# Spreading the operand sums of a Strassen product over the products of the pair before, in one layer of a hybrid decoder

## Chip, core and metric

The kernel runs on one core of a Trainium2 chip. The metric is device time in microseconds, the median of the runs.

## What is computed

One layer of a decoder trunk on 1024 tokens of width 1024, all in float32: two head groups (retention and a delta-rule mixer) behind one input projection, an output projection, a gated feed-forward network, a gated embedding and a final norm. The change lies in the feed-forward part, cut here to what matters:

```python
x = x + mixed @ w_o[i]
hf = rms_norm(x, norm_ffn_w[i])
x = x + (jax.nn.silu(hf @ w_gate[i]) * (hf @ w_up[i])) @ w_down[i]
hp = rms_norm(x, norm_ple_w[i])
x = x + (p[i] @ w_ple_up[i]) * jax.nn.sigmoid(hp @ w_ple_gate[i])
```

The hidden width is 2816, 22 tiles of 128.

## The kernel before

Activations lie transposed, feature by token, in two token halves of 512. For float32 accuracy each operand of a matmul is split into a high part (a copy by ScalarE into the matmul type, L247) and a low part (the operand minus its high part, L248), and every product is three matmuls: high by high, high by low, low by high. Each weight tile is loaded into a stage tile `st` and split into `hi` and `lo`. `dense` (L255) streams the dense projections, of which each step is three matmuls; the function given to it at L1247 says whether VectorE or GpSimd makes the low part of item i.

The feed-forward network of the first token half runs early (`ffn0`) and its hidden tiles go to DRAM (`hd`). For its last two hidden tiles it runs behind the output projection of the second half (`out1`). `norm1` (L1037), called in the evacuation of the first of these gates, takes the norm of the second half: a sum of squares split and multiplied by ones (`nrm`), the square root on ScalarE, the reciprocal on VectorE (L328), and then eight tiles `sq` (L331), each split into `hT1`. `ffn1` then runs gate and up for 22 hidden tiles of the second half.

The product with `w_down` for both token halves is done along the way, two hidden tiles (a pair c) at a time, by Strassen's scheme with seven products, P1 to P7. Its left operands are the four quarter blocks `A` of a pair's `w_down` rows and sums of them (`weights`, L1078, on GpSimd); its right operands are the hidden tiles of the first half, `B[0]` and `B[1]`, loaded from DRAM, those of the second half, `B[2]` and `B[3]`, made by the up products (L1225), and differences of these (`hidden`, L1105, on VectorE; a difference is `sub`, L1076). The split operands lie in eight slots of two `ring` tiles. `unit` (L1119) does a quarter of a product: three matmuls into a PSUM bank `pd`, and an addition by VectorE to the place it belongs to (L1135: `E`, written `rm` in the trace, or the residual `x1`, written `x`). P2, P7 and P3 go on in the bank of the product before them, so their first matmul waits until VectorE has read that bank. For pair 0 ScalarE evacuates P1 and P7 (L1133).

`period` (L1145) lays the units and operands of a pair out in 32 ticks; one tick is taken at each step of `dense`, so that three plain matmuls and three of a product alternate, and the last four ticks hold no product. The 28 units of pair c run in the period of pair c + 1. When the second up product of a pair is done, `hidden(c)` issues all of its differences and splits at once, and the next period begins. `last_period` (L1184) packs the units of the second last pair closer; there `shared` (L1137) adds the sums that several outputs share, behind it `down` multiplies the last pair plainly (L1181) and the gated embedding follows. A scheduler sets the order on each engine from the order in which the program issues instructions and from when their inputs are ready; each engine then works through its own queue in that order.

What the first tick holds, and what a pair ends with:

```python
0: lambda: (dma(out=B[0], in_=hd[f]), dma(out=B[1], in_=hd[f + 1])),
...
while todo:
    tick()
hidden(c)
```

Of the kernel before, what the change touches and what calls it, by code (L numbers as in the profile page):

```python
# [20 lines left out]
KT = 8  # L21
# [85 lines left out]
LEFT = 2  # L107
# [70 lines left out]
def tile_hybrid_layer(ctx: ExitStack, tc: tile.TileContext, I, out):  # L178
# [67 lines left out]
    def split(src, hi, lo, eng=None):  # L246
        act(hi, src, AF.Copy)  # L247
        (eng or V).tensor_tensor(out=lo, in0=src, in1=hi.bitcast(F32), op=ALU.subtract)  # L248
# [81 lines left out]
    def norm_out(raw, w, R, tmp, hi, lo):  # L330
        V.scalar_tensor_tensor(out=tmp, in0=raw, scalar=w, in1=R, op0=ALU.mult, op1=ALU.mult)  # L331
        split(tmp, hi, lo)
# [17 lines left out]
    with ExitStack() as s1:  # L350
# [686 lines left out]
        def norm1():  # L1037
# [3 lines left out]
            for d in range(KT):  # L1041
                norm_out(tail["x1"][d][:, half(1)], pv(NFFN + d), R, tail["sq"](), hT[:, d, 0, :], hT[:, d, 1, :])
# [35 lines left out]
        def weights(c):  # L1078
# [6 lines left out]
            def sums():  # L1085
# [7 lines left out]
                    0: lambda: (dma(out=B[0], in_=hd[f]), dma(out=B[1], in_=hd[f + 1])),  # L1093
                    1: lambda: (part(c, "P1", 0, A[0], G), sums()),
                    3: lambda: sub(G, A[2], A[0], A[2]),
                    5: lambda: part(c, "P2", 0, A[1], G),
                    6: lambda: (part(c, "P1", 1, B[0]), sub(G, A[1], A[1], A[5])),
                    8: lambda: part(c, "P2", 1, B[1]),
# [4 lines left out]
                    26: lambda: part(c, names(c)[6], 0, A[3] if names(c)[6] == "P4" else A[1], G)}  # L1103

        def hidden(c):  # L1105

            B = tail["B"]
            sub(V, B[4], B[2], B[0])
            sub(V, B[5], B[3], B[4])
            part(c, "P6", 1, B[5])  # L1110
            sub(V, B[2], B[3], B[2])
            part(c, "P7", 1, B[2])
            sub(V, B[1], B[5], B[1])
            for n in names(c)[4:]:
                part(c, n, 1, {"P5": B[4], "P3": B[3], "P4": B[1]}[n])

# [20 lines left out]
        def shared(j):  # L1137

            x1, E = tail["x1"], tail["E"]
            V.tensor_tensor(out=E[4 + j], in0=E[4 + j], in1=E[j], op=ALU.add)  # L1140
            V.tensor_tensor(out=x1[j + 4][:, half(0)], in0=x1[j + 4][:, half(0)], in1=E[4 + j], op=ALU.add)
            G.tensor_tensor(out=x1[j][:, half(1)], in0=x1[j][:, half(1)], in1=E[j], op=ALU.add)
            G.tensor_tensor(out=x1[j + 4][:, half(1)], in0=x1[j + 4][:, half(1)], in1=E[4 + j], op=ALU.add)

        def period(c):  # L1145

            ticks = [[] for _ in range(32)]
            if c:
                for u in range(28):
                    ticks[u].append(lambda u=u: unit(c - 1, names(c - 1)[u // 4], u % 4))  # L1150
            for at, fn in weights(c).items():
# [315 lines left out]
```

## Time and profile before

| | |
|---|---|
| median of 3 runs | 1649.02 us (1638.87 to 1649.34) |
| the profiled execution's own time | 1657.07 us |
| its span, first to last instruction | 1655.3 us |
| TensorE matmuls busy | 1511.1 us, 91% |
| VectorE busy | 1240.8 us, 75% |
| ScalarE busy | 729.2 us, 44% |
| GpSimd busy | 532.4 us, 32% |
| DMA, all engines, busiest queue | 36.4% |

Times in the rows are microseconds from the start of the span, unless marked ns. PE is TensorE, DVE VectorE, ACT ScalarE, POOL GpSimd, SP the engine that issues the loads. A name such as `ring<-rm,ring` is what is written and what is read. Idle time before an instruction stands in brackets with what ended it.

### The profile page before, as it was taken

The numbers are of one execution on the slowest core, as the hardware profiler recorded it, in microseconds if no ns is written. First come the engines' busy times: TensorE is split into PE (matmuls) and PEld (weight loads), VectorE is DVE, ScalarE is ACT, GpSimd is POOL, SyncE is SP. The second block draws the span as 40 slices with busy tenths as digits, with TensorE's granted clock in tenths as the row PEclk, the third lists the DMA queues.
The fourth block names the chain that finished last, engine by engine and source line by source line (L and its number), as shares of the span: only waits on it lengthen the run. The fifth ranks groups of instructions, "written<-read, shape, count | busy, mean of one in ns | idle before, by whom it ended". The sixth has DMA issues, their size and how long they took to land.

```text
span 1655.3 us, 21602 instructions
## 1 busy us (share of the span) xinstructions
PE 1511.1 (91%) x7286; PEld 1226.3 (74%) x7286; DVE 1240.8 (75%) x2460; ACT 729.2 (44%) x1451; POOL 532.4 (32%) x404
## 2 busy tenths in 40 slices
PE   6999899998888989889899999999999999998995
PEld 5777778776767767768677777777877777786894
DVE  7669896959798686976855447667777777779877
ACT  6655434434536556263443234533323333333654
POOL 7410111111221123233234314545444445443013
PEclk9999999999999999999999999999999999999997
DMA  6544242334434644243335363322222222322222
GB/s 201 166 169 143 101 132 69 124 115 131 162 117 150 210 152 157 88 142 110 114 123 165 105 189 115 121 90 76 83 77 86 80 76 77 95 72 64 84 74 86
DMA packets 108766, 194.08 MB, mean 117 GB/s; under 512 B 12272, under 2 KB 16496, under 8 KB 108656
## 3 DMA queue, kind: packets, MB, share of 16 engines
q1 hardware_dynamic: 108656, 192.71, 36.4%
q8 instruction: 57, 0.93, 0.2%
q14 instruction: 53, 0.43, 0.1%
HBM read 151.24 MB, written 41.42 MB: 116 GB/s over the span
## 4 chain that ended last, share of the span: by engine, by line
PE 48%; DVE 29%; DMA 8%; ACT 7%; issue 5%; POOL 4%; SPq 0%; DVEq 0%; ACTq 0%; POOLq 0%
PE d L189 26%; PE pd L189 11%; DVE tmp L643 4%; PE pg L189 3%; DVE R L645 3%; POOL lo L248 2%; DVE ring L248 2%; DVE lo L248 2%; DMA st<-in_w_up_dram 1%; DVE rm L1076 1%; ACT hi L247 1%; DMA st<-mixd 1%; DVE Dm L637 1%; DMA st<-in_w_in_dram 1%; DMA st<-in_w_gate_dram 1%
## 5 line engine op out<-in xcount | busy, mean ns | idle before, releaser
L189 PE MATMUL d<-hT,hi 128*128 128x512 f32 x1408 | 460.3, 404 | 9.6 <-DVE g L1011 5.6
L248 POOL TENSOR_TENSOR lo<-st,hi 128x512 fp32r<-128x512 f32 x185 | 261.3, 1414 | 611.2 <-ACT hi L247 552.1
L189 PE MATMUL d<-x,hi 128*128 128x512 f32 x960 | 318.8, 407 | 9.9 <-ACT x L336 8.2
L189 PEld LDWEIGHTS d<-hT,hi 128*128 128x128 f32 x1408 | 266.3, 194 | 62.1 <-ACT hi L247 11.5
L247 ACT ACTIVATE hi<-st 128x512 fp32r<-128x512 f32 x298 | 187.3, 629 | 256.9 <-PE d L189 101.3
L189 PE MATMUL pd<-ring 128*128 128x512 f32 x936 | 270.9, 405 | 26.4 <-DVE rm L1135 23.8
L189 PE MATMUL d<-hT,lo 128*128 128x512 f32 x704 | 281.8, 400 | 2.6 <-POOL lo L248 2.5
L189 PEld LDWEIGHTS pd<-ring 128*128 128x128 f32 x936 | 182.3, 196 | 71.2 <-DVE rm L1135 26.6
L189 PEld LDWEIGHTS d<-x,hi 128*128 128x128 f32 x960 | 176.6, 191 | 44.1 <-ACT x L336 8.2
L189 PE MATMUL d<-x,lo 128*128 128x512 f32 x480 | 192.2, 400 | 2.8 <-POOL lo L248 2.4
L1135 DVE TENSOR_TENSOR x<-x,pd 128x512 f32<-128x512 f32 x200 | 133.5, 683 | 59.4 <-PE pd L189 59.0
L189 PEld LDWEIGHTS d<-hT,lo 128*128 128x128 f32 x704 | 136.2, 193 | 33.4 <-POOL lo L248 4.4
L248 DVE TENSOR_TENSOR lo<-st,hi 128x512 fp32r<-128x512 f32 x113 | 98.5, 872 | 51.2 <-ACT hi L247 50.8
L248 POOL TENSOR_TENSOR ring<-xr,ring 128x512 fp32r<-128x512 f32 x54 | 75.1, 1394 | 182.7 <-ACT ring L247 121.7
L247 ACT ACTIVATE ring<-rm 128x512 fp32r<-128x512 f32 x92 | 57.1, 630 | 145.4 <-PE pd L189 60.3
L189 PEld LDWEIGHTS d<-x,lo 128*128 128x128 f32 x480 | 91.7, 191 | 22.5 <-POOL lo L248 4.3
L643 DVE TENSOR_TENSOR tmp<-Dt,R 128x248 f32<-128x248 f32 (+30 forms) x248 | 88.8, 358 | 3.1
L645 DVE TENSOR_TENSOR R<-R,tmp 128x248 f32<-128x248 f32 (+30 forms) x248 | 86.6, 349 | 3.3
L247 ACT ACTIVATE ring<-xr 128x512 fp32r<-128x512 f32 x54 | 33.6, 628 | 114.6 <-PE pd L189 114.6
L189 PE MATMUL d<-mix,hi 128*128 128x512 f32 x256 | 81.2, 397 | 1.3 <-ACT hi L247 1.3
L248 DVE TENSOR_TENSOR ring<-rm,ring 128x512 fp32r<-128x512 f32 x72 | 74.8, 1073 | 5.5 <-ACT ring L247 4.6
L1135 DVE TENSOR_TENSOR rm<-rm,pd 128x512 f32<-128x512 f32 x72 | 47.6, 681 | 21.5 <-PE pd L189 21.5
(301 smaller groups left out, 2405.2 us busy)
## 6 DMA issues: line engine op xcount, KB each, us to landing
st<-in_w_gate_dram SPq DMA_DIRECT2D x88, 256.0 KB, 2.8
st<-in_w_up_dram SPq DMA_DIRECT2D x88, 256.0 KB, 2.9
st<-in_w_in_dram SPq DMA_DIRECT2D x86, 256.0 KB, 2.8
xr<-in_w_down_dram SPq DMA_DIRECT2D x44, 256.0 KB, 2.6
retd<-rt SPq DMA_DIRECT2D x32, 256.0 KB, 2.7
rr<-retd SPq DMA_DIRECT2D x32, 256.0 KB, 3.3
st<-in_w_o_dram SPq DMA_DIRECT2D x32, 256.0 KB, 2.9
rkvd<-rkvt SPq DMA_DIRECT2D x24, 256.0 KB, 2.1
```

The lines of the kernel that those rows point to most:

```text
L189: return nc.tensor.matmul(ps, lhsT, rhs, start=start, stop=stop, skip_group_check=more)
L247: act(hi, src, AF.Copy)
L248: (eng or V).tensor_tensor(out=lo, in0=src, in1=hi.bitcast(F32), op=ALU.subtract)
L637: V.tensor_tensor(out=Dm, in0=d0v[:, 0].rearrange("p u t -> p t u").unsqueeze(2).broadcast_to([P, 32, 4, NU]), in1=d0v[:, 1].rearrange("p ...
L643: V.tensor_tensor(out=tmp[:, :, 0:i], in0=Dt[:, i:i + 1, 0:i].broadcast_to([P, 8, i]), in1=R[:, :, i:i + 1].broadcast_to([P, 8, i]), op=AL ...
L645: V.tensor_tensor(out=R[:, :, 0:i], in0=R[:, :, 0:i], in1=tmp[:, :, 0:i], op=ALU.subtract)
L1076: eng.tensor_tensor(out=out, in0=x, in1=y, op=ALU.subtract)
L1135: V.tensor_tensor(out=dst, in0=dst, in1=ps, op=ALU.subtract if name == "P4" else ALU.add)
```

## The change

`hidden` returns its parts by tick, and the next period (or, at three quarters of the tick, the last one) issues them between the units. The two hidden tiles of the first half are loaded at ticks 2 and 19 and split at ticks 17 and 28. `shared` is cut in three parts with ticks of their own. In `norm1` GpSimd makes the low part of the seventh tile, and all that period 0 issues on GpSimd is queued behind that instruction (`issue_after`); VectorE and not GpSimd makes the low parts of the weights of the two plain gates and the first gate around it.

```diff
-        (eng or V).tensor_tensor(out=lo, in0=src, in1=hi.bitcast(F32), op=ALU.subtract)
+        return (eng or V).tensor_tensor(out=lo, in0=src, in1=hi.bitcast(F32), op=ALU.subtract)
...
-                norm_out(tail["x1"][d][:, half(1)], pv(NFFN + d), R, tail["sq"](), hT[:, d, 0, :], hT[:, d, 1, :])
+                ins = norm_out(tail["x1"][d][:, half(1)], pv(NFFN + d), R, tail["sq"](), hT[:, d, 0, :], hT[:, d, 1, :], G if d == KT - 2 else V)
+                if d == KT - 2:
+                    tail["held"] = ins.ins
...
-                    0: lambda: (dma(out=B[0], in_=hd[f]), dma(out=B[1], in_=hd[f + 1])),
                     1: lambda: (part(c, "P1", 0, A[0], G), sums()),
+                    2: lambda: dma(out=B[0], in_=hd[f]),
...
-                    6: lambda: (part(c, "P1", 1, B[0]), sub(G, A[1], A[1], A[5])),
-                    8: lambda: part(c, "P2", 1, B[1]),
+                    6: lambda: sub(G, A[1], A[1], A[5]),
+                    17: lambda: part(c, "P1", 1, B[0]),
+                    19: lambda: dma(out=B[1], in_=hd[f + 1]),
...
+                    28: lambda: part(c, "P2", 1, B[1])}
...
-            sub(V, B[4], B[2], B[0])
-            sub(V, B[5], B[3], B[4])
-            part(c, "P6", 1, B[5])
-            sub(V, B[2], B[3], B[2])
-            part(c, "P7", 1, B[2])
-            sub(V, B[1], B[5], B[1])
-            for n in names(c)[4:]:
+            def rest(n):
+                n = names(c)[n]
                 part(c, n, 1, {"P5": B[4], "P3": B[3], "P4": B[1]}[n])
+            return {0: lambda: (sub(V, B[4], B[2], B[0]), sub(V, B[5], B[3], B[4])),
+                    1: lambda: part(c, "P6", 1, B[5]),
+                    2: lambda: sub(V, B[2], B[3], B[2]),
+                    4: lambda: part(c, "P7", 1, B[2]),
+                    5: lambda: sub(V, B[1], B[5], B[1]),
+                    7: lambda: rest(4),
+                    10: lambda: rest(5),
+                    13: lambda: rest(6)}
...
-        def shared(j):
+        def shared(n, j):
             x1, E = tail["x1"], tail["E"]
-            V.tensor_tensor(out=E[4 + j], in0=E[4 + j], in1=E[j], op=ALU.add)
-            V.tensor_tensor(out=x1[j + 4][:, half(0)], in0=x1[j + 4][:, half(0)], in1=E[4 + j], op=ALU.add)
-            G.tensor_tensor(out=x1[j][:, half(1)], in0=x1[j][:, half(1)], in1=E[j], op=ALU.add)
-            G.tensor_tensor(out=x1[j + 4][:, half(1)], in0=x1[j + 4][:, half(1)], in1=E[4 + j], op=ALU.add)
+            if n == 0:
+                G.tensor_tensor(out=x1[j][:, half(1)], in0=x1[j][:, half(1)], in1=E[j], op=ALU.add)
+            elif n == 1:
+                V.tensor_tensor(out=E[4 + j], in0=E[4 + j], in1=E[j], op=ALU.add)
+                V.tensor_tensor(out=x1[j + 4][:, half(0)], in0=x1[j + 4][:, half(0)], in1=E[4 + j], op=ALU.add)
+            else:
+                G.tensor_tensor(out=x1[j + 4][:, half(1)], in0=x1[j + 4][:, half(1)], in1=E[4 + j], op=ALU.add)
...
+                for at, fn in hidden(c - 1).items():
+                    ticks[at].append(fn)
...
+            if held:
+                ticks = [[(lambda fn=fn: with_held(fn, held)) for fn in t] for t in ticks]
...
-                    if 12 <= u < 16:
-                        ticks[k].append(lambda j=u - 12: shared(j))
+                    if 4 <= u < 8:
+                        ticks[k].append(lambda j=u - 4: shared(0, j))
+                    if 13 <= u < 17:
+                        ticks[k].append(lambda j=u - 13: shared(1, j))
+                    if 16 <= u < 20:
+                        ticks[k].append(lambda j=u - 16: shared(2, j))
...
+            for at, fn in hidden(c).items():
+                ticks[at * 3 // 4].append(fn)
...
-                    period(0)
+                    period(0, tail["held"])
...
-                        hidden(c)
...
-        dg = dense(items, count, done, lambda i: G if 0 < i < ntail and (i < EV0 or i % EVM) or i > ntail + KT and i % 2 else V)
+        dg = dense(items, count, done, lambda i: G if 0 < i < ntail and (i < EV0 or i % EVM) or i > ntail + KT + 2 * LEFT + 1 and i % 2 else V)
```

VectorE at the boundary between two pairs, before: `rm<-g,d` is the second up product, `lo` a weight's low part, `rm<-rm` a difference, `ring` an operand's low part, and `pd` an addition of a product.

```order
L1225 TENSOR_TENSOR rm<-g,d 128x512
L248 TENSOR_TENSOR lo<-st,hi 128x512
L1076 TENSOR_TENSOR rm<-rm 128x512 x3
L248 TENSOR_TENSOR ring<-rm,ring 128x512 x4
L1135 TENSOR_TENSOR rm<-rm,pd 128x512
L248 TENSOR_TENSOR lo<-st,hi 128x512
L1135 TENSOR_TENSOR rm<-rm,pd 128x512 x3
```

The same place after the change:

```order
L1252 TENSOR_TENSOR rm<-g,d 128x512
L248 TENSOR_TENSOR lo<-st,hi 128x512
L1144 TENSOR_TENSOR rm<-rm,pd 128x512
L1078 TENSOR_TENSOR rm<-rm 128x512
L1144 TENSOR_TENSOR rm<-rm,pd 128x512
L1078 TENSOR_TENSOR rm<-rm 128x512
L248 TENSOR_TENSOR ring<-rm,ring 128x512
L1144 TENSOR_TENSOR rm<-rm,pd 128x512 x2
L248 TENSOR_TENSOR ring<-rm,ring 128x512
L248 TENSOR_TENSOR lo<-st,hi 128x512
L1144 TENSOR_TENSOR x_9056<-x_9056,pd 128x512 x2
```

The first addition of the new pair stood behind seven differences and low parts; now the weight's low part alone is ahead of it, and the four additions have two differences and one operand's low part between them.

GpSimd around the norm of the second token half, before: `xr` and `rm` are blocks of `w_down` and sums of them, `g` the gate's product with the norm factor.

```order
L248 TENSOR_TENSOR ring<-xr_9057,ring 128x512
L248 TENSOR_TENSOR ring<-xr_9058,ring 128x512
L1086 TENSOR_TENSOR rm<-xr_9059,xr_9060 128x512
L1076 TENSOR_TENSOR rm<-rm,xr_9057 128x512
L1076 TENSOR_TENSOR xr_9059<-xr_9057,xr_9059 128x512
L1076 TENSOR_TENSOR xr_9058<-xr_9058,rm 128x512
L248 TENSOR_TENSOR ring<-rm,ring 128x512
L248 TENSOR_TENSOR lo<-st,hi 128x512 x2
L248 TENSOR_TENSOR ring<-xr_9057,ring 128x512
L1004 TENSOR_TENSOR g<-g,R_6146 128x512
L248 TENSOR_TENSOR lo<-st,hi 128x512 x2
```

After the change, from the split of the norm's tile (`hT_9498`) on:

```order
L248 TENSOR_TENSOR hT_9498<-sq,hT_9498 128x512
L248 TENSOR_TENSOR ring<-xr_9057,ring 128x512
L1088 TENSOR_TENSOR rm<-xr_9059,xr_9060 128x512
L248 TENSOR_TENSOR ring<-xr_9058,ring 128x512
L1078 TENSOR_TENSOR rm<-rm,xr_9057 128x512
L1078 TENSOR_TENSOR xr_9059<-xr_9057,xr_9059 128x512
...
L1004 TENSOR_TENSOR g<-g,R_6146 128x512
L248 TENSOR_TENSOR ring<-rm,ring 128x512
L248 TENSOR_TENSOR ring<-xr_9059,ring 128x512
L248 TENSOR_TENSOR ring<-xr_9058,ring 128x512
L248 TENSOR_TENSOR ring<-xr_9057,ring 128x512
L248 TENSOR_TENSOR lo<-st,hi 128x512
```

The sums and splits of the first pair's weights came ahead of the norm and between the plain gates' low parts; now all thirteen instructions stand between the norm's split and the next weight's low part, the gate's product among them.

TensorE ahead of the first gate on the norm's result (`hT_9498`), before and after, as a difference:

```order
 L189 MATMUL d<-hT_5519,hi 128x512 x2
 L189 MATMUL d<-hT_5519,lo 128x512
-L189 MATMUL pd<-ring 128x512 x3
+L189 MATMUL pd<-ring 128x512 x10
```

Ten matmuls of the first pair's P1, in place of three, are now queued ahead of the first gate.

## Rows read from the trace of the kernel before

**Rows 1.** TensorE's waits, 980 to 1460 us: us in total, times, longest

```profile
PE pd L189 <- DVE rm L1135: 21.8, 8, 2.9
PE d L189 <- DVE g L1011: 5.6, 1, 5.6
```

**Rows 2.** The chain that ended last, 1090 to 1130 us: start, us, what

```profile
1089.87 0.68 PE d L189 x3
...
1099.39 3.42 PE d L189 x15
...
1103.43 1.50 DVE lo L248
1104.93 2.90 DVE rm L1076 x3
1107.83 0.94 DVE ring L248 x2
...
1111.31 0.61 DVE rm L1135
...
1111.96 1.65 PE pd L189 x3
```

**Rows 3.** Busy time in stretches: us, engines' busy us (instructions), granted clock, DMA share, GB/s

```profile
1111.96:1158.52 46.56, 43.95 (x180) 35.78 (x181) 34.62 (x46) 14.39 (x24) 21.17 (x16) 0.94 0.25 80
...
1388.07:1433.39 45.32, 42.50 (x181) 34.75 (x181) 35.02 (x46) 14.38 (x24) 21.18 (x16) 0.97 0.26 82
...
1112.00:1118.00 6.00, 6.00 (x14) 4.76 (x15) 4.58 (x7) 0.63 (x1) 0.43 (x1) 0.50 0.31 90
```

**Rows 4.** VectorE's timeline at the last boundary: start, us, engine, line, operation

```profile
1469.76 1.90 DVE L1076 TENSOR_TENSOR rm<-rm 128x512 f32<-128x512 f32 x3
1471.57 2.50 DVE L248 TENSOR_TENSOR ring<-rm,ring 128x512 fp32r<-128x512 f32 x4
1473.97 1.29 DVE L1135 TENSOR_TENSOR rm<-rm,pd 128x512 f32<-128x512 f32 x2
```

**Rows 5.** GpSimd's timeline at an early boundary and at the last one

```profile
1101.39 1.74 POOL L1076 TENSOR_TENSOR xr<-xr,xr 128x512 f32<-128x512 f32 x1
...
1473.73 3.28 POOL L248 TENSOR_TENSOR ring<-xr,ring 128x512 fp32r<-128x512 f32 x2 [6.14 <-ACT ring L247]
```

**Rows 6.** Timeline of the last pair, VectorE and TensorE

```profile
1492.97 1.76 DVE L1140 TENSOR_TENSOR rm<-rm 128x512 f32<-128x512 f32 x1
...
1495.48 1.72 PE L189 MATMUL pd<-ring 128*128 128x512 f32 x6 [1.81 <-DVE rm L1135]
...
1498.75 2.34 PE L189 MATMUL pd<-ring 128*128 128x512 f32 x6 [0.27 <-DVE x L1135]
1500.93 0.62 PE L189 MATMUL d<-hT,hi 128*128 128x512 f32 x2
...
1515.25 0.96 PE L189 MATMUL pd<-ring 128*128 128x512 f32 x3 [1.24 <-DVE x L1181]
```

**Rows 7.** Timeline of the second half's norm, four engines

```profile
1011.04 1.78 DVE L248 TENSOR_TENSOR ring<-rm,ring 128x512 fp32r<-128x512 f32 x1
...
1015.69 0.63 ACT L247 ACTIVATE ring<-rm 128x512 fp32r<-128x512 f32 x1 [2.86 <-POOL rm L1076]
...
1018.15 0.69 ACT L327 ACTIVATE R<-nrm,par 128x512 f32<-128x512 f32 x1
...
1018.88 3.35 DVE L328 RECIPROCAL R<-R 128x512 f32<-128x512 f32 x1 [0.37 <-ACT R L327]
...
1038.60 1.19 PE L189 MATMUL d<-hT,hi 128*128 128x512 f32 x2 [5.59 <-DVE g L1011]
```

**Rows 8.** The page's costliest groups: busy us, mean ns of one | idle before

```profile
L248 POOL TENSOR_TENSOR lo<-st,hi 128x512 fp32r<-128x512 f32 x185 | 261.3, 1414 | 611.2 <-ACT hi L247 552.1
```

**Rows 9.** VectorE's waits, 1060 to 1460 us: us in total, times, longest

```profile
DVE ring L248 <- ACT ring L247: 3.9, 11, 1.0
```

**Rows 10.** ScalarE's timeline in the last pair

```profile
1498.92 0.63 ACT L247 ACTIVATE ring<-st 128x512 fp32r<-128x512 f32 x1 [9.73 <-DMA st<-in_w_ple_gate_dram]
```

More of the change, by code (lines that the diff above doesn't have):

```diff
@@ L328, in norm_mm, with norm_out @@
         V.reciprocal(out=R, in_=R)
-    def norm_out(raw, w, R, tmp, hi, lo):
+    def norm_out(raw, w, R, tmp, hi, lo, eng=None):
         V.scalar_tensor_tensor(out=tmp, in0=raw, scalar=w, in1=R, op0=ALU.mult, op1=ALU.mult)
-        split(tmp, hi, lo)
+        return split(tmp, hi, lo, eng)
     def raw_split(raw, w, hi, lo):
@@ L1102, in weights @@
                     22: lambda: part(c, names(c)[5], 0, A[1] if names(c)[5] == "P3" else A[4], G),
-                    26: lambda: part(c, names(c)[6], 0, A[3] if names(c)[6] == "P4" else A[1], G)}
+                    26: lambda: part(c, names(c)[6], 0, A[3] if names(c)[6] == "P4" else A[1], G),
+                    28: lambda: part(c, "P2", 1, B[1])}
         def hidden(c):
             B = tail["B"]
-            sub(V, B[4], B[2], B[0])
-            sub(V, B[5], B[3], B[4])
-            part(c, "P6", 1, B[5])
-            sub(V, B[2], B[3], B[2])
-            part(c, "P7", 1, B[2])
-            sub(V, B[1], B[5], B[1])
-            for n in names(c)[4:]:
-                part(c, n, 1, {"P5": B[4], "P3": B[3], "P4": B[1]}[n])
+            def rest(n):
+                n = names(c)[n]
+                part(c, n, 1, {"P5": B[4], "P3": B[3], "P4": B[1]}[n])
+            return {0: lambda: (sub(V, B[4], B[2], B[0]), sub(V, B[5], B[3], B[4])),
[6 more added lines that the diff above has]
+                    13: lambda: rest(6)}
         banks = [None] * 4
@@ L1135, in unit, with with_held, period @@
                 V.tensor_tensor(out=dst, in0=dst, in1=ps, op=ALU.subtract if name == "P4" else ALU.add)
-        def shared(j):
+        def shared(n, j):
             x1, E = tail["x1"], tail["E"]
-            V.tensor_tensor(out=E[4 + j], in0=E[4 + j], in1=E[j], op=ALU.add)
-            V.tensor_tensor(out=x1[j + 4][:, half(0)], in0=x1[j + 4][:, half(0)], in1=E[4 + j], op=ALU.add)
-            G.tensor_tensor(out=x1[j][:, half(1)], in0=x1[j][:, half(1)], in1=E[j], op=ALU.add)
-            G.tensor_tensor(out=x1[j + 4][:, half(1)], in0=x1[j + 4][:, half(1)], in1=E[4 + j], op=ALU.add)
-        def period(c):
+            if n == 0:
[5 more added lines that the diff above has]
+                G.tensor_tensor(out=x1[j + 4][:, half(1)], in0=x1[j + 4][:, half(1)], in1=E[4 + j], op=ALU.add)
+        def with_held(fn, held):
+            with tc.issue_after(held):
+                fn()
+        def period(c, held=None):
             ticks = [[] for _ in range(32)]
```

## The prediction

> **What bounds the kernel now.** I began with what TensorE waits for in the second half of the run, and not with the shares of busy time, since TensorE is busy nearly throughout. From 980 to 1460 us nearly all of its idle time is two entries [rows 1]: eight waits of its Strassen products for VectorE, 21.8 us in all, and one wait of 5.6 us at the second token half's norm. The chain of waits around one of the eight then shows who is late [rows 2]. The products of a pair end at 1102.80. VectorE first makes the low part of a weight tile, then three operand differences, then four low parts of operands, and only at 1111.31 does it add the first product of the new pair to its sum. The matmul that accumulates onto that PSUM bank starts at 1111.96. In clean stretches three matmuls take 0.68 us, 0.2267 us each; after the wait three took 1.65 us. The busy time in stretches says why [rows 3]: from 1112 to 1118 the granted clock is 0.50, the lower of the two levels (1.2 of 2.4 GHz), after about 3 us in which TensorE did almost nothing. So each of the eight waits is paid twice, as idle time and as slow matmuls.
>
> **The pair boundaries.** The eight stalls stand at a pitch of (1433.39 - 1111.96) / 7 = 45.92 us (starts of the seven stretches, first and last in [rows 3]). One pitch holds 180 matmuls; at 0.2267 us that is 40.8. A boundary thus costs 5.1 us: 2.7 of waiting (21.8 / 8) and 2.4 of slow clock.
>
> The change puts additions of products between the operand differences, as the order of VectorE's rows shows. I lay the new row out from 1103.43 with the durations of the old block, the stretched ones: low part of weights until 1104.93; addition 0.61 (1105.54); difference 2.90 / 3 = 0.97 (1106.51); addition (1107.12); difference (1108.09); operand low part (1111.31 - 1107.83) / 4 = 0.87 (1108.96); two additions (1109.57 and 1110.18) [rows 2]. TensorE's need: the first new product starts at about 1102.7, the product that accumulates on it is 24 matmuls later, 1108.2, the next three follow each 1.36 later (1109.6, 1110.9, 1112.3). The four additions are early by 2.7, 2.5, 1.3 and 2.1 us. All four stalls in the row vanish with their cause, and so does the clock loss behind them: 8 x 5.1 = 41 us. What is late next is the third addition, with 1.3 us left.
>
> The same work remains: three differences and four low parts a boundary, some 6 us, now beside the products. VectorE is busy 34.6 of 46.56 us in a pair [rows 3], which in 40.8 us is 85%; there is room, but less. The last boundary before shows that the block itself is not long: at 1469.76 to 1473.97 the seven instructions took 4.2 us, 0.60 each, and no stall followed [rows 4]. GpSimd was idle there (until 1473.73 for 6.14 us), while at 1101.39 it was in the midst of its sums, that one 1.74 us long [rows 5]. So the block of 2.90 + 3.48 = 6.4 us is long because both engines work out of SBUF at once, and the new row is laid out with that already in it.
>
> Here a rule speaks against the change. The Trainium skill, "SBUF — State Buffer", section "Who interferes with whom", says that a VectorE instruction with two SBUF inputs contends with a GpSimd instruction that reads SBUF, that whoever issues first keeps the port, and that the other is blocked until it ends. The row bears it out in part: 0.60 alone, 0.87 to 0.97 in the block. By the rule in full each of the new row's SBUF steps could wait out one GpSimd instruction; that is the first rival below.
>
> The loads of the hidden tiles move from the start of a pair to its third and twentieth slot, and their splits to the 18th and 29th. Nine slots of 1.36 us (three plain matmuls and three of a product) lie between the second load and its split, 12 us, and eight more before its reader; I cost them at nothing. On the load queue they change places by one load. If that cover were gone, the splits' copies would hold ScalarE's queue; this is the last rival.
>
> **The last pair.** Its products are packed closer, and shared sums run on VectorE and GpSimd together: a VectorE sum takes 1.76 us there. TensorE waits 1.81 us at 1495.48, and its next 6 + 3 + 6 = 15 matmuls take until 1500.93, 5.45 us where 3.40 would do [rows 6]. The change has half of GpSimd's sums done eight products earlier. Four VectorE sums at 1.76 would lose up to 4 x 1.16 us, more than the wait. I take 1.81 + 2.05 = 3.9 us as gain; the bounds are 0 (contention as it was) and 8 (the waits from 1515 on go too).
>
> **The norm of the second half.** Before, GpSimd sums operands while VectorE works towards the norm: a VectorE instruction of the 0.60 kind takes 1.78, ScalarE waits 2.86 us for a GpSimd difference ahead of the square root's table load, the square root runs at 1018.15 and the reciprocal at 1018.88; the first gate starts at 1038.60 after 5.59 us idle [rows 7]. After the change all of GpSimd's sums queue behind one split of the norm (the order of GpSimd's rows). Without the 2.86 us the reciprocal can start about 2.4 us earlier. VectorE gets four more low parts of weights and gives up one of the norm, so 3 x 0.60 = 1.8 us more, and is no longer stretched. TensorE, meanwhile, finds ten matmuls of the first product ahead of the gate, not three (the order of TensorE's rows): seven matmuls, 1.6 us, are done in idle time, but the ninth waits for GpSimd's second instruction behind the norm. From the reciprocal at 1016.4 to the product that frees the gate's bank VectorE has 3.35 + 21 x 0.60 = 16.0 us, 1032.4, and weight tiles it must await put about 1 us on that; GpSimd's split, two places earlier, ends about 1033.8, its next instruction 1035.3, and the matmuls behind it let the gate start at about 1036.2. That is a gain of 2.4 + 1.6 = 4.0.
>
> The price follows. In GpSimd's queue 13 instructions now stand between the norm's split and the low part of the second gate's weights. At their mean of 1.41 us [rows 8] that is 18.4 us from about 1033.8, and with the low part itself 1053.6. TensorE needs it 48 matmuls and 2 us of slow clock after 1036.2, plus the two that need only the high part: 1049.5. So 4 us of waiting, with some slow clock behind it as in [rows 3]. Bounds: 1.29 us each and no clock loss, about 2.5 us; 1.74 each and the clock loss too, 8.7 + 2.4. Against 4.0 gained, the stage lies between 4 us faster (if the queue's waits fall elsewhere) and 7 us slower; I take 1 us slower.
>
> **Sum.** -41 - 3.9 + 1 = -44 us on the profiled execution's own time of 1657.07 (span 1655.3), which gives 1613. The runs shown have a median of 1649.02, 8 us below it. The stalls sit in every execution of the same queues, so I take the 44 us off the median: 1605.
>
> **The rivals.**
> - The third addition becomes the new wait. For it: 1.3 us is thin, and a VectorE sum beside a busy GpSimd took 1.76 [rows 6]. With 1.7 for two differences and one low part the third addition ends at 1109.57 + 0.73 + 0.73 + 0.83 = 1111.9, 1.0 late. The clock would mostly hold: after a wait of 1.24 us at 1515.25 three matmuls took 0.96 us, not 1.65 [rows 2, 6]. Eight times 1.0, and a second wait of that size a pair, is 16: 1621; with the clock lost at every one, 8 x (1.0 + 2.4) = 27: 1632. Against it: the block of before has the contention in it already. By that rule of the Trainium skill, if it holds at every step, the time is this one.
> - GpSimd's queue behind the norm is the late one: the stage comes out 7 us slower in place of 1, and the boundaries still go: 1611. For it: 13 instructions in a row, where before they stood in groups with the low parts of weights between them. Against it: VectorE, which stretches them, has little to do from 1036 to 1050.
> - The change doesn't do what it says: the additions come early, but the wait moves to a later product whose operand is now split slots later, and TensorE stalls as long there. About 1645. Against it: operands come 1.4 to 12 us ahead of their slots in the new row.
> - Slower: VectorE's queue is held by one operand copy. Each low part now stands between additions and waits for its ScalarE copy, and ScalarE works in order behind weight copies that wait for loads, one of them 9.73 us [rows 10]. Nothing can be added meanwhile. It decides from 1.3 + 5.1 = 6.4 us of hold in each pair; at 9.73 a pair loses 8.4 + 2.4 - 5.1 = 5.7 us, eight of them 46: 1695. Against it: in 400 us VectorE waited for such copies 11 times, 1.0 us at most [rows 9].
>
> **How the numbers follow.** Forecast 0.70, the thin margin 0.14, GpSimd's queue 0.08, a moved wait 0.05, slower 0.03. The forecast's own range, from the bounds of the last pair and of the norm, is 1596 to 1616, and the runs of before differ by 10 us. The range 1592 to 1624 takes in GpSimd's queue and the thin margin where the clock holds. A measurement of this kernel tells about 1%, 16 us, from no change. Faster by more takes the forecast, GpSimd's queue and most of the thin margin: 0.90. Within 1%: the moved wait and the thin margin's end, 0.07. Slower: 0.03.
>
> **What would show it.** Right: no wait for VectorE at the eight boundaries, a pitch of 41 us from pair to pair with the granted clock at 1.00 through it, and additions between the differences. At the norm the reciprocal near 1016 and the first gate near 1036, then a wait of some 4 us for a GpSimd low part about 1050. In the last pair no wait of 1.8 us ahead of the first late product. Wrong: a pitch above 43 us, a wait in each pair for an addition or an operand, or a norm that loses more than 7 us.

## The result and the profile after

The changed kernel takes 1618.78 us (median of four runs, 1617.30 to 1624.83) beside 1644.84 for the kernel before in the same series. By the medians that is 26.1 us less; by the ratio, 0.9851 with a 95% interval of 0.9803 to 0.9899, it is 24.5. The forecast was 44: the predicted 1605 is 14 us too low, and 1618.78 lies in the range of 1592 to 1624. The profiled execution took 1624.83 us (span 1623.1). One later run of the changed kernel took 3193.45 us, twice the others, and is left out of its ratio.

TensorE's largest waits of the changed kernel, 980 to 1430 us (us in total, times, longest), which answer to [rows 1]:

```profile
PE pd L189 <- POOL ring L248: 4.5, 1, 4.5
PE d L189 <- POOL lo L248: 1.8, 1, 1.8
PE d L189 <- DVE lo L248: 1.2, 1, 1.2
```

All eight waits for an addition of products are gone, and so is the wait of 5.6 us at the norm. Three waits at the norm stand in their place, two of them for GpSimd.

Two of the eight pairs in the view by stretches, the first and the last (columns as in [rows 3]):

```profile
1109.34:1150.14 40.80, 40.80 (x181) 33.78 (x180) 32.64 (x45) 14.12 (x25) 20.86 (x16) 1.00 0.29 91
...
1395.00:1435.80 40.80, 40.80 (x182) 33.78 (x181) 31.48 (x44) 12.73 (x23) 17.90 (x14) 1.00 0.32 98
```

A pair takes 40.80 us with TensorE busy for all of it and the granted clock at 1.00, where before had 46.56 and 45.32 at 0.94 and 0.97 [rows 3]. This is the pitch that was forecast from 180 matmuls of 0.2267 us.

VectorE and then GpSimd in the changed kernel, at the boundary of 1150 us (start, us, engine, line, operation):

```profile
1150.75 1.25 DVE L248 TENSOR_TENSOR lo<-st,hi 128x512 fp32r<-128x512 f32 x1
1151.92 0.67 DVE L1144 TENSOR_TENSOR rm<-rm,pd 128x512 f32<-128x512 f32 x1
1152.52 1.18 DVE L1078 TENSOR_TENSOR rm<-rm 128x512 f32<-128x512 f32 x1
1153.62 0.67 DVE L1144 TENSOR_TENSOR rm<-rm,pd 128x512 f32<-128x512 f32 x1
1154.22 0.68 DVE L1078 TENSOR_TENSOR rm<-rm 128x512 f32<-128x512 f32 x1
1154.82 0.68 DVE L248 TENSOR_TENSOR ring<-rm,ring 128x512 fp32r<-128x512 f32 x1
1155.42 1.27 DVE L1144 TENSOR_TENSOR rm<-rm,pd 128x512 f32<-128x512 f32 x2
1156.62 1.38 DVE L248 TENSOR_TENSOR ring<-rm,ring 128x512 fp32r<-128x512 f32 x1
1157.92 1.77 DVE L248 TENSOR_TENSOR lo<-st,hi 128x512 fp32r<-128x512 f32 x1
```

```profile
1150.15 1.30 POOL L248 TENSOR_TENSOR ring<-xr,ring 128x512 fp32r<-128x512 f32 x1
1151.40 1.75 POOL L248 TENSOR_TENSOR lo<-st,hi 128x512 fp32r<-128x512 f32 x1
1156.16 1.29 POOL L248 TENSOR_TENSOR ring<-xr,ring 128x512 fp32r<-128x512 f32 x1 [3.01 <-ACT ring L247]
1157.53 1.61 POOL L1078 TENSOR_TENSOR xr<-xr,rm 128x512 f32<-128x512 f32 x1
```

Set side by side, the two lists show what sets a VectorE duration. The step at 1152.52 starts while GpSimd's instruction of 1151.40 runs, which ends at 1153.15, and it ends 0.55 us later, at 1153.70. The same 0.55 stands behind GpSimd's ends at 1151.45, 1157.45 and 1159.14. A step that meets no GpSimd instruction takes 0.68 (0.60 from one start to the next). Over the eight pairs of this trace all 55 steps with both inputs in SBUF that start while a GpSimd instruction runs end 0.54 to 0.55 us behind it, and the 16 that start shortly before one take 0.68 to 0.69. The additions, with one operand in PSUM, take 0.67 also beside GpSimd: the one at 1151.92 lies wholly within the GpSimd instruction of 1151.40.

The whole run in stages, from the starts of four VectorE instructions: the eighth residual addition of the second half's output projection, the fourth and the twentieth up product (the first boundary and the last one, eight pairs apart), and the reciprocal behind the last pair. The runs repeated later (below) stand beside the first ones:

| us | before | before, again | after | after, again |
|---|---|---|---|---|
| up to the end of the output projection | 1008.1 | 1007.0 | 1011.2 | 1004.0 |
| norm of the second half and first pair | 94.7 | 94.7 | 98.1 | 98.6 |
| eight pairs | 365.7 | 355.2 | 326.5 | 326.5 |
| last pair, up to the reciprocal | 60.2 | 59.6 | 60.8 | 60.8 |
| the rest | 126.6 | 127.0 | 126.4 | 126.4 |
| span | 1655.3 | 1643.5 | 1623.1 | 1616.3 |

From profile to profile the eight pairs lost 39.3 us, 41 forecast. The norm's stage grew by 3.4, forecast 1. The last pair grew by 0.7, where 3.9 were to be gained. The first stage, which the change doesn't touch, differs by 7 us between two executions of the changed kernel, so kernels that differ by a few us are compared by the stages behind it.

The norm of the second half in the changed kernel: TensorE, GpSimd, and VectorE, whose rows answer to [rows 7]:

```profile
1039.70 0.73 PE L189 MATMUL pd<-ring 128*128 128x512 f32 x2 [4.50 <-POOL ring L248]
1040.26 0.82 PE L189 MATMUL d<-hT,hi 128*128 128x512 f32 x2
...
1051.91 0.50 PE L189 MATMUL d<-hT,lo 128*128 128x512 f32 x1 [1.24 <-DVE lo L248]
...
1056.77 0.50 PE L189 MATMUL d<-hT,lo 128*128 128x512 f32 x1 [1.82 <-POOL lo L248]
```

```profile
1036.20 1.66 POOL L248 TENSOR_TENSOR hT<-sq,hT 128x512 fp32r<-128x512 f32 x1 [10.06 <-ACT hT L247]
1037.82 1.82 POOL L248 TENSOR_TENSOR ring<-xr,ring 128x512 fp32r<-128x512 f32 x1
...
1048.79 1.28 POOL L1004 TENSOR_TENSOR g<-g,R 128x512 f32<-128x512 f32 x1
...
1055.47 1.25 POOL L248 TENSOR_TENSOR lo<-st,hi 128x512 fp32r<-128x512 f32 x1
```

```profile
1011.20 0.69 DVE L1033 TENSOR_TENSOR x<-xr,d 128x512 f32<-128x512 f32 x1 [1.54 <-PE d L189]
...
1019.13 3.35 DVE L328 RECIPROCAL R<-R 128x512 f32<-128x512 f32 x1 [1.20 <-ACT R L327]
...
1050.11 0.69 DVE L1011 SCALAR_TENSOR_TENSOR g<-g,d 128x512 f32<-128x512 f32 x1 [6.19 <-POOL g L1004]
1050.71 1.15 DVE L248 TENSOR_TENSOR lo<-st,hi 128x512 fp32r<-128x512 f32 x1
```

GpSimd works without a gap from 1036.20 to 1056.7. Each of TensorE's three waits ends with something that stood in this queue: the low part of P1's left operand (ended 1039.64), the gate's product of 1048.79, for which VectorE stood 6.19 us before it could make a weight's low part, and the weight's low part of 1055.47.

The last pair in the changed kernel, ScalarE, VectorE and TensorE:

```profile
1456.15 0.63 ACT L247 ACTIVATE ring<-st 128x512 fp32r<-128x512 f32 x1 [5.30 <-DMA st<-in_w_ple_gate_dram]
1456.69 1.14 ACT L247 ACTIVATE ring<-rm 128x512 fp32r<-128x512 f32 x2
```

```profile
1457.34 1.97 DVE L248 TENSOR_TENSOR ring<-rm,ring 128x512 fp32r<-128x512 f32 x2 [3.82 <-ACT ring L247]
1459.22 1.27 DVE L1144 TENSOR_TENSOR rm<-rm,pd 128x512 f32<-128x512 f32 x2
```

```profile
1459.95 0.98 PE L189 MATMUL pd<-ring 128*128 128x512 f32 x3 [1.71 <-DVE rm L1144]
...
1465.45 1.62 PE L189 MATMUL pd<-ring 128*128 128x512 f32 x6 [1.76 <-DVE rm L1144]
```

ScalarE's copy of a gate weight waits 5.30 us for its load; behind it stand the copies of the last two hidden tiles, behind these VectorE's low parts of them, 3.82 us idle, and behind these the additions that TensorE needs.

### The profile page after: what moved, and what is told of

It reads as the page before. It is cut to its first block, busy times and chain, and to the rows that moved or that the text cites. A ratio compares the mean times of both kernels' runs of the same rounds, so it can differ in the third digit from the quotient of the medians.

```text
span 1623.1 us, 21604 instructions
## 1 busy us (share of the span) xinstructions
PE 1497.5 (92%) x7286; PEld 1217.7 (75%) x7286; DVE 1220.1 (75%) x2463; ACT 724.8 (45%) x1451; POOL 525.1 (32%) x401
## 4 chain that ended last, share of the span: by engine, by line
PE 44%; DVE 23%; issue 8%; DMA 5%; ACT 5%; POOL 3%; SPq 0%; DVEq 0%; ACTq 0%; POOLq 0%
PE d L189 24%; PE pd L189 11%; PE pg L189 3%; DVE tmp L643 3%; DVE R L645 3%; POOL lo L248 1%; DMA st<-in_w_up_dram 1%; DMA st<-in_w_gate_dram 1%; DVE lo L248 1%; DMA st<-mixd 1%; DVE Dm L637 1%; ACT hi L247 1%; POOL ring L248 1%; DVE STb L749 1%; DMA st<-in_w_in_dram 1%
## 5 line engine op out<-in xcount | busy, mean ns | idle before, releaser
L189 PE MATMUL d<-hT,hi 128*128 128x512 f32 x1408 | 452.0, 401 | 3.6 <-ACT hi L247 3.6
L248 POOL TENSOR_TENSOR lo<-st,hi 128x512 fp32r<-128x512 f32 x181 | 255.0, 1411 | 602.3 <-ACT hi L247 535.5
L189 PE MATMUL pd<-ring 128*128 128x512 f32 x936 | 260.7, 391 | 12.7 <-POOL ring L248 4.5
L189 PEld LDWEIGHTS pd<-ring 128*128 128x128 f32 x936 | 174.7, 188 | 53.8 <-POOL ring L248 4.9
L189 PEld LDWEIGHTS d<-x,hi 128*128 128x128 f32 x960 | 178.3, 193 | 43.9 <-ACT x L336 8.1
L248 DVE TENSOR_TENSOR lo<-st,hi 128x512 fp32r<-128x512 f32 x117 | 105.1, 898 | 54.3 <-ACT hi L247 52.2
L248 DVE TENSOR_TENSOR ring<-rm,ring 128x512 fp32r<-128x512 f32 x72 | 64.1, 893 | 24.8 <-ACT ring L247 24.1
L1004 POOL TENSOR_TENSOR g<-g,R 128x512 f32<-128x512 f32 x22 | 29.1, 1325 | 109.7 <-DVE g L1003 107.0
```

The lines of the kernel that those rows point to most:

```text
L189: return nc.tensor.matmul(ps, lhsT, rhs, start=start, stop=stop, skip_group_check=more)
L248: return (eng or V).tensor_tensor(out=lo, in0=src, in1=hi.bitcast(F32), op=ALU.subtract)
L1004: G.tensor_tensor(out=g, in0=g, in1=R0[0], op=ALU.mult)
```

## The experiments

Two things were to be explained: why the timed gain is about 25 us and not 44, and what the norm's edits and the last pair cost. The theories: the slow clock behind the eight waits, which I read from one execution, is not the same in every one; GpSimd's held queue costs more than the earlier norm gives; one copy behind a load took the last pair's gain. The rivals stand with each run.

**The kernel before, once more** (no edit).

> The kernel before, unchanged, profiled once more. If a boundary costs the same in every execution, the eight pairs from the fourth to the twentieth up product take 365.7 us again, with eight waits of 2.7 us and a granted clock of 0.94 to 0.97 in the pairs. If the waits are the same but the clock lost behind them differs from one execution to the next (my theory of why the timed gain is 26 us and not 44), the eight waits come out at 21 to 22 us again, while the eight pairs take anything between 348 us (8 x (40.8 + 2.7)) and 366, and among the timed runs the longer spans go with the lower clocks.

It took 1643.73 us (ten runs, 1637.33 to 1648.87), and 23 runs of the kernel before beside it 1634.81 to 1649.45: none as long as the 1657.07 of the execution that I had read. Among these 33 runs the longer ones have the lower clock, as expected: granted over the whole run were 0.981 to 0.984 in the five shortest, 0.974 to 0.978 in the five longest, and 0.970, less than in any of them, in the execution that I had read. The eight waits came out at 20.7 us in all, 21.8 before, but the eight pairs at 355.2 us and not 365.7. The views below show, of the new execution, its first two pairs and two slices of 2 us behind its first wait, which ended at 1110.6; then, of the execution read ahead of the prediction, the first and the third such slice behind its first wait, which ended at 1112.0:

```profile
1101.72:1146.73 45.01, 42.42 (x181) 34.73 (x180) 34.54 (x45) 14.38 (x25) 21.19 (x16) 0.96 0.26 82
1146.73:1190.72 43.99, 41.40 (x181) 33.63 (x180) 34.34 (x45) 14.38 (x25) 21.10 (x16) 1.00 0.27 84
...
1110.60:1112.60 2.00, 1.99 (x5) 1.62 (x6) 2.00 (x3) 0.00 (x0) 0.49 (x1) 0.50 0.50 139
1112.60:1114.60 2.00, 2.00 (x9) 1.60 (x8) 1.73 (x4) 0.63 (x1) 0.00 (x0) 0.78 0.44 131
```

```profile
1112.00:1114.00 2.00, 2.00 (x5) 1.62 (x6) 2.00 (x3) 0.11 (x1) 0.43 (x1) 0.50 0.48 143
...
1116.00:1118.00 2.00, 2.00 (x6) 1.62 (x5) 1.20 (x2) 0.00 (x0) 0.00 (x0) 0.50 0.00 0
```

The wait is much the same (2.82 us in the first profile, 2.59 in the second), what follows is not. In the first profile the clock stayed at 0.50 for 6 us, in the second it rose within 4. In five of the second's eight pairs, at 43.9 to 44.1 us each, the granted clock over the pair is 1.00; in the other three, at 45.0 to 45.1, it is 0.96. A boundary costs 45.7 - 40.8 = 4.9 us in the one and 355.2 / 8 - 40.8 = 3.6 in the other; both hold 2.6 to 2.7 of waiting, so the slow clock took 2.2 and 1.0. Against this second execution the change is worth 28.8 us at the boundaries (355.2 and 326.5) and, with +3.4 at the norm, +1.3 in the last pair and -0.6 behind it, 24.6 behind the output projection, which is the timed gain. What in an execution decides for how long the clock stays low isn't shown by these runs.

**The spread alone.** The changed kernel without the norm's edits, and with the shared sums as before:

```diff
-                ins = norm_out(..., G if d == KT - 2 else V)
+                ins = norm_out(..., V)
-                    period(0, tail["held"])
+                    period(0)
-        dg = dense(items, count, done, lambda i: ... or i > ntail + KT + 2 * LEFT + 1 and i % 2 else V)
+        dg = dense(items, count, done, lambda i: ... or i > ntail + KT and i % 2 else V)
```

> The kernel before with the spread alone: the operand differences and low parts in slots of the next pair, the two hidden-tile loads moved, the shared sums and the norm stage as before. Theory (the boundaries are the whole gain and need nothing of the norm's edits): all eight waits gone, 326 us from the fourth to the twentieth up product, the norm stage at 94.7 us give or take 1 (eighth product of the output projection to the fourth up product), the time 3 us under the changed kernel. Rival (GpSimd's order behind the norm has its part in it): a pair above 42 us or a wait left in the early pairs, and a time over that of the changed kernel.

TensorE's two largest waits in it, 980 to 1460 us:

```profile
PE d L189 <- DVE g L1011: 5.6, 1, 5.6
PE pd L189 <- DVE rm L1142: 4.4, 2, 2.2
```

No boundary waits (the two of 2.2 us lie in the last pair), the eight pairs take 326.5 us, the norm's stage 95.3, the last pair 59.9. The time is 1611.84 us, ratio 0.9823 (0.9790 to 0.9856). Behind the output projection it takes 608.0 us, 3.8 less than the changed kernel, where 3 were expected. So the boundaries are the whole gain, and the spread needs none of the norm's edits for it.

**The norm's edits alone,** on the kernel before: the three lines of the diff above the other way round.

> The kernel before with the norm's edits alone: GpSimd's operand work held behind the split of the norm, that split on GpSimd, the first four weight low parts on VectorE; the block at the boundaries as before. Theory (thirteen held instructions in GpSimd's queue cost more than the earlier square root gives): the norm stage takes 98 us where before took 94.7, with waits of TensorE for GpSimd of 4 and 2 us about 1035 to 1060, and the eight waits of 2.7 us stay. Rival (the 3.4 us come from the spread, whose loads and splits moved in the first pair): 93 to 95 us.

TensorE's three largest waits in it, 980 to 1460 us:

```profile
PE pd L189 <- DVE rm L1137: 20.7, 8, 2.7
PE pd L189 <- POOL ring L248: 4.5, 1, 4.5
PE d L189 <- POOL lo L248: 3.4, 2, 1.8
```

The stage takes 99.1 us, and the ratio is 1.0025 (1.0005 to 1.0046): the edits cost some 4 us by themselves, though the reciprocal comes 7.93 us behind the residual addition, 2.8 sooner than the 10.76 of the kernel before. The rival, that the spread's moved loads cost this, falls: here nothing is spread.

**GpSimd taken out of the boundary.** The kernel before; left out from the third pair on are GpSimd's two sums, two differences and the low parts of two left operands, so this kernel no longer computes the layer.

```diff
-                    1: lambda: (part(c, "P1", 0, A[0], G), sums()),
-                    3: lambda: sub(G, A[2], A[0], A[2]),
-                    5: lambda: part(c, "P2", 0, A[1], G),
-                    6: lambda: (part(c, "P1", 1, B[0]), sub(G, A[1], A[1], A[5])),
+                    1: lambda: (part(c, "P1", 0, A[0], G if c < 2 else None), sums() if c < 2 else None),
+                    3: lambda: sub(G, A[2], A[0], A[2]) if c < 2 else None,
+                    5: lambda: part(c, "P2", 0, A[1], G if c < 2 else None),
+                    6: lambda: (part(c, "P1", 1, B[0]), sub(G, A[1], A[1], A[5]) if c < 2 else None),
```

> The kernel before, with GpSimd's two sums, two differences and the low parts of two left operands left out from the third pair on (six of some ten instructions of GpSimd about each boundary); VectorE's block keeps its eight instructions. Theory (the block is long because GpSimd's instructions stretch it): the block shrinks from 7.8 to about 5.7 us, the waits from 2.7 to 0.5 us, the clock holds at 1.00 behind them, and a pair falls from 45.7 to 41 to 42 us from the third boundary on. Rival (eight instructions ahead of the first addition are too many by themselves): waits stay above 2 us and a pair above 44.

VectorE at the first boundary of it, and the pair that begins there:

```profile
1096.48 0.69 DVE L248 TENSOR_TENSOR lo<-st,hi 128x512 fp32r<-128x512 f32 x1
1097.09 1.89 DVE L1079 TENSOR_TENSOR rm<-rm 128x512 f32<-128x512 f32 x3
1098.89 2.50 DVE L248 TENSOR_TENSOR ring<-rm,ring 128x512 fp32r<-128x512 f32 x4
1101.30 0.68 DVE L1138 TENSOR_TENSOR rm<-rm,pd 128x512 f32<-128x512 f32 x1
```

```profile
1095.88:1136.83 40.95, 40.95 (x181) 33.70 (x180) 30.41 (x46) 14.63 (x25) 11.98 (x9) 1.00 0.31 91
```

The same eight instructions, in the old order ahead of the first addition, now take 4.8 us (1096.48 to 1101.30), 0.60 each, and not 7.9 (1103.43 to 1111.31, [rows 2]), and no wait follows, here or at the other seven boundaries: 40.95 us a pair at a clock of 1.00. Its time of 1611.20 us, ratio 0.9821 (0.9776 to 0.9865), is that of the spread. Eight instructions were not too many; GpSimd's work beside them made them late. In the kernel before, three of the eight (the weight's low part, the first difference and the last low part) end 0.55 us behind a GpSimd instruction, and the other five go at 0.60. The Trainium skill, "SBUF — State Buffer", section "Who interferes with whom", says that a VectorE instruction with two SBUF inputs contends with a GpSimd instruction that reads SBUF, that the port pair which they share is an exclusive lock, and that a VectorE instruction with at most one SBUF input does not contend. The rows agree: 0.60 alone, an end 0.55 us behind GpSimd's end where GpSimd had begun first, and 0.67 for the additions out of PSUM in either case.

**The norm's stage mended,** on the changed kernel: P1's left operand isn't held, the last plain gates' product and the first six weight tiles' low parts are VectorE's.

```diff
-                    1: lambda: (part(c, "P1", 0, A[0], G), sums()),
+                    1: lambda: (part(c, "P1", 0, A[0], G) if c else None, sums()),
+                ticks[1].insert(0, lambda: part(c, "P1", 0, tail["A"][0], G))
-                G.tensor_tensor(out=g, in0=g, in1=R0[0], op=ALU.mult)
+                (G if f < NF - LEFT else V).tensor_tensor(out=g, in0=g, in1=R0[0], op=ALU.mult)
-        ... i > ntail + KT + 2 * LEFT + 1 and i % 2 else V)
+        ... i > ntail + KT + 2 * LEFT + 5 and i % 2 else V)
```

> The changed kernel with its norm stage mended: the low part of the first left operand no longer held behind the norm; the last gate products' scaling by R0 and the low parts of the first six weight tiles on VectorE. Theory (what the norm stage lost, it lost to the held queue of GpSimd): TensorE's waits of 4.50 us for a GpSimd operand, 1.24 and 1.82 us for low parts of weights go, and the stage falls from 98.1 us to 90 to 92, under the 94.7 of before, since the square root stays 2.8 us earlier. Rival (the first half of the second gate waits for VectorE's norm chain whatever GpSimd does): the waits are renamed to VectorE and the stage stays at 95 or more.

TensorE's two largest waits in it, 980 to 1440 us, and a row of ScalarE:

```profile
PE d L189 <- ACT hi L247: 3.5, 2, 2.9
PE d L189 <- DVE lo L248: 1.5, 1, 1.5
```

```profile
1050.06 0.63 ACT L247 ACTIVATE hi<-st 128x512 fp32r<-128x512 f32 x1 [6.37 <-DMA st<-in_w_gate_dram]
```

The waits for GpSimd are gone and the stage falls to 94.0 us, under before and short of the 90 to 92 expected: the next wait, 2.9 us, is for a weight tile whose load came late. The theory holds in its sign and in four of its six to eight us. The time is 1618.10 us, ratio 0.9836 (0.9799 to 0.9872), not to be told from the changed kernel's: the last pair and the rest take 62.4 and 127.4 us there, 2.6 more together than in the changed kernel. The waits of the last pair are the same as there, but its matmuls take 53.2 us, at a granted clock of 0.95, and not 51.6 at 1.00; behind it they take 1.0 us more. Why the clock was lower is open.

**The last pair mended,** on the changed kernel:

```diff
-            ticks[11].append(lambda: tail["gate_weights"](1))
+            ticks[14].append(lambda: tail["gate_weights"](1))
```

> The changed kernel with the first load of the last gate's weights asked for three slots later in the last pair, so that ScalarE copies the last hidden tiles before, and not after, a copy that waits for that load. Theory (one operand copy held behind a load wait is why the last pair gained nothing): TensorE's waits of 1.71 and 1.76 us for additions go, and the stretch from the twentieth up product to the reciprocal falls from 60.9 us to 57 to 58. Rival (the shared sums on VectorE and GpSimd set the pace): waits of about that size stay, at other products, and the stretch stays at 60 or more.

TensorE's waits in it, 1440 to 1490 us:

```profile
PE pd L189 <- DVE x L1144: 2.6, 4, 1.1
PE pd L189 <- DVE x L1202: 2.2, 1, 2.2
PE nrm L189 <- ACT sq L247: 2.0, 1, 2.0
```

The waits of 1.71 and 1.76 us are gone, others of up to 2.2 us stand at later products, and the stretch takes 59.0 us, 1.9 less, where 3 to 4 were expected. Both sides have a part in it: the held copy was real, and behind it TensorE waits for VectorE's additions. The time of 1618.16 us, ratio 0.9836 (0.9804 to 0.9867), can't be told from the changed kernel's.

**Both mends, and the spread with the last pair's mend alone.** The second is the changed kernel with the diff above and without the norm's edits.

> Both mends together on the changed kernel. If both theories hold: norm stage 90 to 92 us, last stretch 57 to 58, eight pairs 326.5 as before, the time 8 to 10 us under the changed kernel, about 1609. If neither: within 2 us of the changed kernel.

> The changed kernel without its norm edits, and with the last pair mended. If the norm edits as they stand are a loss of 3 us and the mend a gain of 3: 5 to 6 us under the changed kernel, about 1612 less the last pair's share, 1609 to 1612, and norm stage 95 us. If the spread of the shared sums itself costs in the last pair, its last stretch stays at 60 us or more, against 59.9 of the spread alone.

Both mends: 1612.23 us, ratio 0.9794 (0.9766 to 0.9822), with 93.8 us at the norm, 59.8 in the last pair and 127.0 behind it. The spread with the last mend: 1611.22 us, ratio 0.9799 (0.9770 to 0.9828), with 94.6, 59.0 and 126.3. From the end of the output projection on that is 607.1 and 606.4 us against the changed kernel's 611.8. Both mends together gain 4.8 there and not 8 to 10, since neither stage came down as far as expected; the spread with the last mend came out as expected in its time, its norm and its last pair.

**The changed kernel beside the better one, and the shared sums.** Three runs of one series: the changed kernel again, the spread with the last mend again, and the latter with the shared sums in their old order:

```diff
-                    if 4 <= u < 8:
-                        ticks[k].append(lambda j=u - 4: shared(0, j))
-                    if 13 <= u < 17:
-                        ticks[k].append(lambda j=u - 13: shared(1, j))
-                    if 16 <= u < 20:
-                        ticks[k].append(lambda j=u - 16: shared(2, j))
+                    if 12 <= u < 16:
+                        ticks[k].append(lambda j=u - 12: (shared(1, j), shared(0, j), shared(2, j)))
```

> The changed kernel once more, on the chip of the two runs beside it. Norm stage 98 us, eight pairs 326.5, last stretch 60.9, the time 1617 to 1621; if the norm edits are a loss of some 3 us and the last pair's hold one of 2, it comes out 5 us over the kernel without both, in the same series.

> The spread without the norm's edits and with the last pair mended, repeated beside the changed kernel: 1611 to 1614, 5 us or so under it, with norm stage 94.6, pairs 326.5 and last stretch 59.0.

> The same, with the shared sums in the order of the kernel before (all four of a column together, with the fourth product). If the earlier start of half of GpSimd's sums is worth what I forecast for the last pair (3.9 us), the last stretch comes out at 62 to 63 us. If the sums' order is worth nothing and only the held operand copy counted, 58.5 to 59.5.

The changed kernel: 1618.04 us, ratio 0.9843 (0.9818 to 0.9868). The spread with the last mend: 1611.96, ratio 0.9822 (0.9790 to 0.9855), norm 95.3, last pair 59.0. By the stages behind the output projection it is 5.1 us ahead (612.2 and 607.1); the intervals of the timed ratios overlap, so the times alone point the same way twice and settle no size.

With the shared sums as before the last pair takes 60.0 us: the sums' earlier start is worth 1.1 us at most, not 3.9. At most, because TensorE's idle time in the stretch is 6.6 us with the late sums and 6.8 with the early ones; what differs is the time of its matmuls, 53.4 and 52.2 us at a granted clock of 0.94 and 0.97, in one execution. The runs also show that the mend and the sums hang together:

| last pair, us | sums as before | sums early |
|---|---|---|
| copies held behind the load | 59.9 (the spread alone) | 60.8, 60.8 (the changed kernel) |
| load asked for later | 60.0 | 59.0, 59.0 (the spread with the last mend) |

The mend's 1.9 us are there only with the early sums, and without the mend the early sums cost about 1. With the sums as before the mend changes nothing, so something else holds up the pair there, the late sums perhaps; the left column is one execution each, so this is not shown. The last run's time of 1617.16 us, ratio 0.9840 (0.9814 to 0.9866), is 5 us over the other's, 4 more than its stages explain; its first stage, on the same code, was 1009.6 and not 998.3 us in the profiles, so no more is read from it.

## Why the prediction was right, and where it was wrong

- **What bounds the kernel: right.** The eight waits were for VectorE's block of operand differences and low parts, and they went when additions came between them. That the block was long because of GpSimd, which I argued from the last boundary [rows 4, 5], is now shown: without GpSimd's work the old order doesn't wait either.
- **The new row: right.** It was to have its additions early by 2.7, 2.5, 1.3 and 2.1 us. In the rows of 1150 us the first product starts at 1149.94, so TensorE needs the additions from 1155.38 on, each 1.36 later; they end at 1152.59, 1154.29, about 1156.05 and 1156.69, which is early by 2.8, 2.4, 2.0 and 2.8. The other seven boundaries agree within 0.2 us. The third is the thinnest, as forecast, and 40.80 us is the pitch. The durations that it was laid out with were mixtures of 0.60 and some 1.7 (see the last section), so that the row came this close is partly luck.
- **The term that was mis-sized: 8 x 5.1 = 41 us.** Its 2.7 of waiting was right. Its 2.4 of slow clock was one execution's (2.2 with the eighth pair, 44.28 us, which the pitch over seven starts leaves out); another had 1.0. The step that failed is "the stalls sit in every execution of the same queues, so I take the 44 us off the median". It holds for the waits, not for the clock behind them, and the profile warned of it: the profiled execution was 8 us over the median and longer than every run shown. With 1.0 the term is 8 x 3.7 = 30 us, and the forecast 1649 - 30 - 3.9 + 1 = 1616.
- **The last pair: wrong in sign.** Forecast -3.9, measured +0.7 (+1.3 against the second run of before), and two waits of 1.71 and 1.76 us stand where none of 1.8 was to be. Two steps failed. The earlier sums were priced by the 1.16 us that four VectorE sums were stretched; they gave 1.1 at most. And I worked out what the spread does at the boundaries only: in the last pair its slots put the hidden tiles' copies behind a gate weight's load, which cost the changed kernel 1.9 us. This is the mechanism of my slower rival, at one place in place of eight; [rows 10] had shown that load's wait in that very pair.
- **The norm: +1 forecast, +3.4 and +3.9 measured,** inside the bounds of -4 to +7. The reciprocal came 2.8 us sooner (2.4 forecast). The first gate started 1040.26 - 1011.20 = 29.1 us behind the residual addition, 30.5 before, and seven matmuls of 0.2267 us were done ahead of it: 3.0 gained, 4.0 forecast. From that start to the stage's end it took 69.1 us, 64.2 before; with the seven matmuls, which no longer stood in it, that is a price of 6.4, forecast 5. The waits behind the gate were 1.24 + 1.82, not 4. Of the rest, 3.4, the clock has some 1.4: in the trace 17 matmuls of that stretch are at 0.43 us, 10 before. The others are the restarts behind the two waits, 0.3 each, and four short stops between 1069 and 1088, 0.3 to 0.5 each, for which there is no forecast. VectorE was to be idle at that time, and was, but it stood behind the one gate's product that was left in GpSimd's queue. The stretch from the first gate to the end of the stage, of the changed kernel and then of the kernel before (columns as in [rows 3]):

```profile
1040.26:1109.34 69.08, 65.56 (x268) 51.89 (x267) 36.27 (x46) 29.02 (x51) 42.29 (x32) 0.95 0.31 100
```

```profile
1038.60:1102.83 64.23, 64.23 (x274) 53.03 (x275) 37.12 (x51) 29.27 (x51) 33.57 (x25) 0.97 0.36 111
```

- **The rivals.** The thin third addition didn't come, though the rule that I had set beside it held at every step. The price took all three operand steps ahead of it as stretched to 1.7 us; in the rows GpSimd is idle for 3.01 us ahead of 1156.16, so one of the three is blocked (1.18) and two take 0.68, and the additions, which TensorE awaits, aren't blocked. The slower rival's threshold of 6.4 us of hold left out the 2.4 us of slow clock that its price has; with it, it is 4.0. GpSimd's queue behind the norm came at half its price. No wait moved to a later product within the eight pairs.
- **The range: luck.** The forecast's own range was 1596 to 1616 (its bounds add up to 1615), and 1618.78 lies above it. It lies in the wider range because that took in the thin margin, which didn't come. The start was off as well: the 1649.02 of three runs became 1644.84 with a fourth, and later series had medians of 1641 to 1646. From 1645 the corrected term gives 1612, and the 4.6 us missed in the last pair and the 2.4 at the norm bring it to 1619.

## What to carry to other kernels

A wait and the slow clock behind it are two terms: here the wait repeated from one execution to the next, the slow stretch did not. When the profiled execution is longer than the timed runs, read the second term as an upper bound. Where a VectorE block is late, look at what GpSimd does in the same microseconds before you reorder it. And work out a change of order at the ends of the loop too: here one slot table served eight places well and cost at the ninth. Where two things may hold up the same stretch, as in the last pair, test them together as well as one by one.

## What the runs showed of the hardware that I had not expected

- After a first wait of 2.82 us in one execution and 2.59 in another the granted clock stayed at 0.50 (1.2 of 2.4 GHz) for 6 us in the one and rose within 4 in the other, and over five of eight pairs of that other it was 1.00, after waits of 2.5 to 2.6 us.
- A VectorE step with both inputs in SBUF isn't stretched in proportion beside GpSimd: if it starts while a GpSimd instruction runs, it ends 0.55 us behind that (55 of 55 steps over the eight pairs). My means of 0.87 and 0.97 us [rows 2] were averages over 0.60 and some 1.7.
- Up to the end of the output projection two executions of the changed kernel differ by 7 us (1011.2 and 1004.0), and three kernels that share this stage, in one series, by 11 (998.3 to 1009.6): more than several of the edits here are worth.
